# Splitting each weight once and keeping the split copy in DRAM scratch

## The chip, the cores and the metric

The kernel runs on one core of a Trainium2 chip. The metric is device time in microseconds (us). Three executions of the kernel before took 1098.61, 1100.31 and 1105.79 us; the median is 1100.31 us.

## What is computed

One encoder layer over two groups of tokens, a prompt of 1024 and a sample of 512, with 1024 channels each. Cut to what matters:

```python
h = rmsnorm(x, norm_g)
z = h @ w_in                                   # 1024 -> 4096 channels
hy_in, hy_gate, att_qkv, att_gate = split(z)
x0, x1, vv = split(short_conv(hy_in))
y_hy  = x0 * long_conv(x1 * vv, kfilt, hy_bias)            # FFT convolution
y_hy  = rmsnorm(y_hy, on_hy) * silu(hy_gate)
y_att = neighbourhood_attention(rmsnorm(q), rmsnorm(k), v, rpb)
y_att = rmsnorm(y_att, on_att) * silu(att_gate)
return x + concatenate([y_hy, y_att]) @ w_out
```

Both groups go through the same weights `w_in` and `w_out`, so every piece of a weight is used twice.

## The kernel before

TensorE multiplies in fp32r, a rounded float32. To keep float32 accuracy each operand is split into `hi` (the rounded value) and `lo` (what rounding left, rounded in turn), and each product is three matmuls: hi·hi, hi·lo, lo·hi. Weights arrive in pieces of [128, 1024] float32 (512 KB): 20 pieces of `w_ch` (channel-major projections, L392), 12 of `w_tk` (token-major ones, L405) and 8 of `w_out` (L1111). Each piece is split into two units, each a pair of tiles `whi`, `wlo` of [128, 512].

For each unit `issue_w` rounds half of the raw piece into `whi` (L365) and GpSimd subtracts `whi` from the raw half into `wlo` (L366). Rounding is done on ScalarE for the prompt (`self.w_round`), and on VectorE from the sample on. A pool has 2 raw buffers and 4 of `whi` and of `wlo`. `fetch_w` loads the raw piece behind the next one ahead of time. Since a piece is used once for the prompt and once for the sample, it is loaded and split twice: 80 loads, 160 roundings, 160 subtractions.

The work comes in five phases. `plan` fixes from the counts of steps how generators take turns, and with that the order of the weights: (1) filters' spectra beside q, k, v of the prompt; (2) hyena of the prompt; (3) attention of the prompt beside all projections and hyena of the sample; (4) output projections of the prompt and the first half of the sample's, beside the attention of the sample; (5) the second half of the sample's output. In the profile phase 3 takes about 535 to 885 us, phases 4 and 5 the time from there. In phase 4 `out_part` runs as `out0` and `out1` for the prompt and `out0` for the sample, four pieces of `w_out` each, and from `more_w` on the units come from two pools in turn. Within each phase a scheduler with a timing model of its own sets the order of instructions on each engine. Every DMA is issued by SyncE (SP) in that order and on one queue: an issue that waits holds up all behind it.

Other lines that come up: T and Ti are the bias tables of the attention, summed on GpSimd (L63) from `qkr`, which is loaded from `in_rpb`; `hThi_s`, `hTlo_s` are the sample's operands, loaded at the start of phase 3; L79 is a multiplication by a scalar on VectorE.

Of the kernel before, what the change touches and what calls it, by code (L numbers as in the profile page):

```python
# [49 lines left out]
class Kernel:  # L50
# [6 lines left out]
    # ---------------------------------------------------------------- helpers  # L57
# [28 lines left out]
    def psum(self, side, keep=0, **banks):  # L86
        """Share the banks of one side out anew, but for its first keep pools: tag -> number of banks."""
# [11 lines left out]
    # ------------------------------------------------------------------ setup  # L99
    def setup(self):  # L100
# [6 lines left out]
        self.w_pos, self.w_raw, self.w_ready, self.w_bufs = 0, [], [], 4  # L107
        self.dr = ctx.enter_context(self.pool("dr", space=bass.MemoryType.DRAM))
# [19 lines left out]
        # DRAM scratch  # L128
# [57 lines left out]
    def stack(self, out, src):  # L186
        """The halves of the partitions of src, split: hi in their own place and lo on the other half."""
        for d in range(2):
            r, o = slice(d * 64, d * 64 + 64), slice(64 - d * 64, 128 - d * 64)
            self.nc.scalar.copy(out=out[d][r], in_=src[r])  # L190
            self.sub(out[d][o], src[r], f32(out[d][r]))

    def w3_load(self, pool):
        """The last weights of the filters: per half of the partitions hi on both halves, and lo in its place."""
# [8 lines left out]
    def rsqrt(self, pool, ss, n, scale, name):  # L203
        """(ss * scale + eps) ** -0.5 for a [P, n] tile."""
# [13 lines left out]
    # ------------------------------------------------------------ input norm  # L218
    def x_norm(self, G, xp, ahead):
        """The rows of x, scaled by their rms."""  # L220
# [18 lines left out]
    def x_turn(self, G, hps):  # L239
        """Channel-major copies of the normed x, split into hi and lo."""  # L240
# [12 lines left out]
    def x_pre(self, G, pool):  # L253
        """Channel-major copies of the normed x, split into hi and lo, to scratch."""
# [39 lines left out]
    # --------------------------------------------------------------- weights  # L294
    def steps(self, what):
        """The pieces of the weights that each step of a generator takes."""
# [19 lines left out]
    def merge(ns, spans):  # L316
        """The order in which generators of ns[i] steps take turns, each spread evenly over its span."""
# [3 lines left out]
    def plan(self, phases):  # L321
        """phases: lists of (names of chained generators, span, priority).  Sets the order of the weights."""
# [9 lines left out]
    def weave(self, *gens):  # L332
        """Trace the generators of the next phase in turns."""
# [10 lines left out]
    def fetch_w(self):  # L344
        """Load the next [P, 1024] piece."""
        if self.w_pos < len(self.w_seq):
# [3 lines left out]
            raw = pool.tile([P, 1024], F32, name="wraw", bufs=2)  # L350
            self.dma(raw, self.io[key[0]][key[1:]])
            self.w_raw.append((key, raw, pool))

    def issue_w(self):
        """Split the next piece into two units of (hi, lo) [P, 512]; the piece behind it is on its way."""
        nc = self.nc
        if not self.w_raw:
            self.fetch_w()
        key, raw, pool = self.w_raw.pop(0)
        self.fetch_w()  # L360
        for u in range(2):
            hi = pool.tile([P, 512], F32R, name="whi", bufs=4)
            lo = pool.tile([P, 512], F32R, name="wlo", bufs=4)
            r = raw[:, u * 512:(u + 1) * 512]
            next(self.w_round)(out=hi, in_=r)  # L365
            nc.gpsimd.tensor_tensor(out=lo, in0=r, in1=f32(hi), op=ALU.subtract)  # L366
            self.w_ready.append((key, hi, lo))

    def take_w(self, key):
        """The next unit of piece key; pieces behind it are fetched as far as there is room."""  # L370
# [8 lines left out]
    def proj_ch(self, G, *gis):  # L379
        """128 output channels of each granule of gis, channel-major: per granule a list of psum [P, 512].  # L380
        The granules take turns in each segment of tokens."""
# [13 lines left out]
    def proj_tok(self, gi, hi, lo, nt):  # L395
        """256 output columns, token-major, for nt (<=8) token tiles.  Returns list of psum [P, 4, 256]."""
# [1005 lines left out]
```

## Time and profile before

| | |
|---|---|
| runs | 1098.61, 1100.31, 1105.79 us, median 1100.31 us |
| profiled execution, first to last instruction | 1101.3 us (the only time recorded for it) |
| PE busy | 1030.7 us, 94% |
| DVE, ACT, POOL busy | 824.4, 561.1, 539.9 us |
| moved by DMA | 154.87 MB, mean 141 GB/s |
| mean granted TensorE clock | 0.987 |

PE is TensorE, DVE VectorE, ACT ScalarE, POOL GpSimd, SPq the queue of SyncE. PE is busy nearly throughout, so what a change to the other engines is worth is found in the gaps of PE: what each gap waits for, and how the granted clock moves around it.

### The profile page before, as it was taken

What the parts mean: (1) busy time and instruction counts of PE and PEld (TensorE: products, weight loads), DVE (VectorE), ACT (ScalarE), POOL (GpSimd) and SP (SyncE); (2) the same over time, 40 slices, a digit from 0 to 9 for tenths busy, and PEclk for the clock granted to TensorE, in tenths of its full rate; (3) what the DMA queues carried; (4) which work ended last, traced back from release to release, by engine and by line L of the source; (5) the groups of instructions that cost most, each with busy time, mean ns of one, the idle gap of its engine ahead of it and who ended that gap; (6) DMA issues with size and microseconds to landing.
All of it is one profiled execution on the core that took longest, in us unless ns stands there. A gap on an engine that the chain in (4) does not pass through costs nothing. (4 is left out here: it accounts for less than half of the span.)

```text
span 1101.3 us, 18549 instructions
## 1 busy us (share of the span) xinstructions
PE 1030.7 (94%) x6492; PEld 895.6 (81%) x6492; DVE 824.4 (75%) x2098; ACT 561.1 (51%) x1223; POOL 539.9 (49%) x480
## 2 busy tenths in 40 slices
PE   3999898998999999999898999999999999899998
PEld 2888887987888878787786887888777798798898
DVE  5988679456148597868768898999886868966874
ACT  6644616444534343443425577667567764564530
POOL 2133636325245474545445645455455564766452
PEclk9999999899999999999999899999999999999999
DMA  9134461645612121122375244445544376966522
GB/s 343 34 122 144 143 207 61 219 150 164 224 39 74 46 79 54 50 72 77 118 227 173 78 129 146 120 141 182 140 129 138 114 243 190 321 203 205 164 76 89
DMA packets 110780, 154.87 MB, mean 141 GB/s; under 512 B 7793, under 2 KB 80315, under 8 KB 109919
## 3 DMA queue, kind: packets, MB, share of 16 engines
q1 hardware_dynamic: 110687, 153.69, 44.3%
q8 instruction: 51, 0.84, 0.3%
q14 instruction: 42, 0.34, 0.1%
HBM read 110.35 MB, written 43.32 MB: 140 GB/s over the span
## 5 line engine op out<-in xcount | busy, mean ns | idle before, releaser
L366 POOL TENSOR_TENSOR wlo<-wraw,whi 128x512 fp32r<-128x512 f32 x160 | 231.5, 1451 | 308.4 <-ACT whi L365 180.7
L392 PE MATMUL bank<-hThi_p,whi 128*128 128x512 f32 x320 | 125.2, 391 | 2.0 <-DVE cx L75 2.0
L392 PE MATMUL bank<-hTlo_p,whi 128*128 128x512 f32 x320 | 125.5, 392 | 0.0
L392 PE MATMUL bank<-hThi_p,wlo 128*128 128x512 f32 x320 | 125.4, 392 | 0.0
L405 PE MATMUL bank<-whi,hThi_p 128*128 128x256 f32 x384 | 110.4, 290 | 2.5 <-ACT qsq L849 2.0
L1111 PE MATMUL bank<-whi,hi 128*128 128x256 f32 x384 | 111.0, 291 | 0.8 <-ACT hi L1090 0.5
L405 PE MATMUL bank<-wlo,hThi_p 128*128 128x256 f32 x384 | 110.8, 291 | 0.0
L1111 PE MATMUL bank<-wlo,hi 128*128 128x256 f32 x384 | 110.0, 288 | 0.0
L1111 PE MATMUL bank<-whi,lo 128*128 128x256 f32 x384 | 109.5, 289 | 0.3 <-POOL lo L63 0.3
L405 PE MATMUL bank<-whi,hTlo_p 128*128 128x256 f32 x384 | 108.1, 289 | 0.0
L450 POOL TENSOR_TENSOR Z<-zc,Z 128x256 fp32r<-128x256 f32 x80 | 69.5, 878 | 49.2 <-ACT Z L449 36.2
L1002 ACT ACTIVATE s_sb<-s_sb,mx 128x360 f32<-128x360 f32 (+1 forms) x96 | 60.4, 629 | 63.6 <-DVE mx L998 63.0
L405 PEld LDWEIGHTS bank<-whi,hThi_p 128*128 128x128 f32 x384 | 74.2, 194 | 4.9 <-ACT qsq L849 2.4
L1111 PEld LDWEIGHTS bank<-whi,hi 128*128 128x128 f32 x384 | 73.4, 191 | 4.1 <-issue 2.1
L405 PEld LDWEIGHTS bank<-wlo,hThi_p 128*128 128x128 f32 x384 | 74.5, 194 | 1.6 <-issue 0.7
L1111 PEld LDWEIGHTS bank<-wlo,hi 128*128 128x128 f32 x384 | 73.6, 192 | 1.6 <-issue 1.6
L1111 PEld LDWEIGHTS bank<-whi,lo 128*128 128x128 f32 x384 | 73.1, 192 | 1.7 <-issue 1.1
L405 PEld LDWEIGHTS bank<-whi,hTlo_p 128*128 128x128 f32 x384 | 73.3, 194 | 1.2 <-issue 0.7
L392 PEld LDWEIGHTS bank<-hThi_p,whi 128*128 128x128 f32 x320 | 60.3, 188 | 14.0 <-DVE cx L75 2.4
L392 PEld LDWEIGHTS bank<-hTlo_p,whi 128*128 128x128 f32 x320 | 60.4, 189 | 11.3
L392 PEld LDWEIGHTS bank<-hThi_p,wlo 128*128 128x128 f32 x320 | 60.3, 188 | 11.3
L392 PE MATMUL bank<-hThi_s,whi 128*128 128x512 f32 x160 | 64.6, 407 | 4.4 <-DVE cvv L75 2.3
(292 smaller groups left out, 3108.4 us busy)
## 6 DMA issues: line engine op xcount, KB each, us to landing
wraw<-in_w_ch_dram SPq DMA_DIRECT2D x40, 512.0 KB
wraw<-in_w_tk_dram SPq DMA_DIRECT2D x24, 512.0 KB
wraw<-in_w_out_dram SPq DMA_DIRECT2D x16, 512.0 KB
V<-v_p SPq DMA_DIRECT2D x32, 240.0 KB
v_p<-vg SPq DMA_DIRECT2D x32, 160.0 KB
K_p<-Kw SPq DMA_DIRECT2D x4, 1088.0 KB
x<-in_x_prompt_dram SPq DMA_DIRECT2D x8, 512.0 KB
dec<-in_dec_p_dram SPq DMA_DIRECT2D x16, 256.0 KB
```

The lines of the kernel that those rows point to most:

```text
L366: nc.gpsimd.tensor_tensor(out=lo, in0=r, in1=f32(hi), op=ALU.subtract)
L392: nc.tensor.matmul(ps, lhsT=w, rhs=h[s][:, k], start=(k == 0 and i == 0), stop=(k == KC - 1 and i == 2))
L405: nc.tensor.matmul(pss[t // 2][:, t % 2, :], lhsT=h[t // 4][:, k, t % 4 * P:(t % 4 + 1) * P], rhs=w, start=(k == 0 and i == 0 and t % 2 == ...
L450: nc.gpsimd.tensor_tensor(out=Z[:, 1, 0:2, :], in0=z, in1=f32(Z[:, 0, 0:2, :]), op=ALU.subtract)
L1002: nc.scalar.activation(out=s_sb[:, :n], in_=s_sb[:, :n], func=AF.Exp, bias=mx, scale=-1.0, accum_out=l)
L1111: nc.tensor.matmul(ps[:, j, :], lhsT=h[:, tok], rhs=w, start=(k == 0 and i == 0 and j == 0), stop=(k == 3 and i == 2 and j == 1))
```

## The change

At the first use of a piece each unit is split as before, now into the two halves of one tile `wsp` [128, 2, 512], and that tile is also written to a DRAM tile `ws_...` of 512 KB, if the piece comes again. At the second use no raw piece is loaded: each unit is loaded ready from its DRAM tile, into buffers of tag `wsp` or, every third, `wraw`. So a pool holds 4 units at first use and 6 at second use; `w_bufs`, which limits how far `take_w` runs ahead, goes from 4 to 6 with phase 3 and from 8 to 10 in phase 4. In numbers: 80 subtractions on GpSimd and 80 roundings (78 on VectorE, 2 on ScalarE) go; 40 loads of 512 KB become 80 loads of 512 KB; 80 stores of 512 KB are added, 64 of them before phase 3 and 16 from its end on.

```diff
     def fetch_w(self):
...
-            raw = pool.tile([P, 1024], F32, name="wraw", bufs=2)
-            self.dma(raw, self.io[key[0]][key[1:]])
+            raw = None
+            if key not in self.w_split:
+                raw = pool.tile([P, 1024], F32, name="wraw", bufs=2)
+                self.dma(raw, self.io[key[0]][key[1:]])
             self.w_raw.append((key, raw, pool))
 
     def issue_w(self):
...
         key, raw, pool = self.w_raw.pop(0)
+        kept = self.w_split.get(key)
+        if kept is None:
+            kept = self.w_split[key] = [self.dr.tile([P, 2, 512], F32, name="_".join(["ws", *map(str, key), str(u)])) for u in range(2)]
         self.fetch_w()
         for u in range(2):
-            hi = pool.tile([P, 512], F32R, name="whi", bufs=4)
-            lo = pool.tile([P, 512], F32R, name="wlo", bufs=4)
-            r = raw[:, u * 512:(u + 1) * 512]
-            next(self.w_round)(out=hi, in_=r)
-            nc.gpsimd.tensor_tensor(out=lo, in0=r, in1=f32(hi), op=ALU.subtract)
-            self.w_ready.append((key, hi, lo))
+            if raw is None:
+
+                tag = next(self.w_tags.setdefault(id(pool), itertools.cycle(["wsp", "wsp", "wraw"])))
+                t = pool.tile([P, 2, 512], F32R, name=tag, bufs=2 if tag == "wraw" else 4)
+                self.dma(f32(t), kept[u])
+            else:
+                t = pool.tile([P, 2, 512], F32R, name="wsp", bufs=4)
+                r = raw[:, u * 512:(u + 1) * 512]
+                next(self.w_round)(out=t[:, 0], in_=r)
+                self.nc.gpsimd.tensor_tensor(out=t[:, 1], in0=r, in1=f32(t[:, 0]), op=ALU.subtract)
+                if key in self.w_seq[self.w_pos:]:
+                    self.dma(kept[u], f32(t))
+            self.w_ready.append((key, t[:, 0], t[:, 1]))
...
         self.w_round = itertools.repeat(self.nc.vector.tensor_copy)
+        self.w_bufs = 6
...
-            self.w_pools, self.w_bufs = itertools.cycle((wp, self.wp)), 8
+            self.w_pools, self.w_bufs = itertools.cycle((wp, self.wp)), 10
```

The other lines of the diff only drop comments. The scheduler makes a new order of it. Three places in it matter below. The first is on GpSimd near the start of phase 3, where the first bias tables are summed; before:

```order
L63 TENSOR_TENSOR cx_6422<-cx_6422,cvv 128x512
L366 TENSOR_TENSOR wlo<-wraw,whi 128x512 x3
L63 TENSOR_TENSOR T_6350<-cmask,qkr 128x480
L63 TENSOR_TENSOR T_6353<-cmask,qkr 128x480
L63 TENSOR_TENSOR Ti_6352<-T_6350,rmask 128x480
L63 TENSOR_TENSOR Ti_6355<-T_6353,rmask 128x480
L366 TENSOR_TENSOR wlo<-wraw,whi 128x512
L470 TENSOR_TENSOR Z<-zc,Z 128x256
```

There a weight's subtraction stands behind four sums of the tables. The same place after:

```order
L63 TENSOR_TENSOR cx_6478<-cx_6478,cvv 128x512
L63 TENSOR_TENSOR T_6406<-cmask,qkr 128x480
L63 TENSOR_TENSOR T_6409<-cmask,qkr 128x480
L483 TENSOR_TENSOR Z<-zc,Z 128x256
L463 TENSOR_TENSOR Z<-zc,Z 128x256
L63 TENSOR_TENSOR Ti_6408<-T_6406,rmask 128x480
```

The tables remain, and no work on weights stands behind them. The second place is the queue of SP at the change from phase 2 to 3, up to the first loads of the sample's operands (`Kc` are spectra of filters, `ga_p` gates that are stored); before:

```order
L60 DMA wraw<-in_w_tk_dram 128x1024
L60 DMA Kc<-K_p_93 128x256
L60 DMA wraw<-in_w_tk_dram 128x1024
L60 DMA Kc<-K_p_93 128x256 x4
L60 DMA hThi_s<-hT_76 128x1024
L60 DMA ga_p_89<-vg 128x1024
L60 DMA hTlo_s<-hT_77 128x1024
```

Two raw pieces stand well ahead of the sample's operands. The same place after:

```order
L60 DMA wsp<-ws_w_ch_0_3311 128x1024
L60 DMA wsp<-ws_w_ch_1_3312 128x1024
L60 DMA Kc<-K_p_93 128x256 x3
L60 DMA wsp<-ws_w_tk_0_1_190 128x1024
L60 DMA Kc<-K_p_93 128x256
L60 DMA wsp<-ws_w_tk_1_0_240 128x1024
L60 DMA hThi_s<-hT_76 128x1024
L60 DMA ga_p_89<-vg 128x1024
L60 DMA hTlo_s<-hT_77 128x1024
```

Four loads of units, each into a buffer that TensorE must have left, are now mixed into the last loads ahead of them. The third place is the queue of SP in phase 4 around the loads of the sample's rows (`acc`) and of the prompt's partial sums (`oy`); before:

```order
L60 DMA wraw<-in_w_out_dram 128x1024 x2
L60 DMA ox<-in_x_prompt_dram 128x2x256
L60 DMA V<-v_s_122 120x3x128
L60 DMA qkr<-in_rpb_dram 128x1x488
L60 DMA ox<-in_x_prompt_dram 128x2x256
L60 DMA lo_12507<-A_s_105 128x512
L60 DMA acc<-in_x_sample_dram 128x4x256 x4
```

After, at the same loads:

```order
L60 DMA ws_w_out_0_0_10839<-wsp 128x1024
L60 DMA sum<-oo 128x2x256
L60 DMA acc<-in_x_sample_dram 128x4x256 x3
L60 DMA qkr<-k_s_120 128x4x128
L60 DMA acc<-in_x_sample_dram 128x4x256
L60 DMA ws_w_out_0_1_10840<-wsp 128x1024
L60 DMA wraw<-in_w_out_dram 128x1024
L60 DMA oy<-sum 128x2x256
L60 DMA ox<-in_x_prompt_dram 128x2x256
L60 DMA wsp<-ws_w_out_0_0_10378 128x1024
L60 DMA wsp<-ws_w_out_0_1_10379 128x1024
```

Stores of units, each behind its own subtraction, now stand among the loads, and units of the second use are fetched there too.

## Rows read from the trace of the kernel before

**Rows 1.** The page, part 1: busy us, share of the span, instructions.

```profile
PE 1030.7 (94%) x6492; PEld 895.6 (81%) x6492; DVE 824.4 (75%) x2098; ACT 561.1 (51%) x1223; POOL 539.9 (49%) x480
```

**Rows 2.** Windows by stage: length, busy PE, PEld, DVE, ACT, POOL; clock, DMA share, GB/s.

```profile
0.00:535.00 535.00, 493.74 (x2970) 430.02 (x2971) 370.51 (x963) 246.88 (x550) 235.36 (x206) 0.99 0.36 119
535.00:885.00 350.00, 333.44 (x1989) 277.98 (x1988) 299.28 (x759) 217.28 (x452) 183.31 (x164) 0.98 0.49 147
885.00:1101.30 216.30, 203.53 (x1536) 187.55 (x1534) 154.64 (x378) 96.90 (x222) 121.20 (x112) 0.99 0.60 184
```

**Rows 3.** Lines L365 and L366: durations in ns, min/median/max, first and last start.

```profile
L365 DVE CAST whi<-wraw x94: 398/422/1560, 536.9 to 1074.3; 128x512 fp32r<-128x512 f32 x94
...
L366 POOL TENSOR_TENSOR wlo<-wraw,whi x160: 1261/1296/5379, 10.9 to 1075.8; 128x512 fp32r<-128x512 f32 x160
```

**Rows 4.** Windows of line L365 alone: length, busy DVE, busy ACT; clock, DMA share, GB/s.

```profile
535.00:885.00 350.00, 39.88 (x66) 0.00 (x0) 0.98 0.49 147
885.00:1101.30 216.30, 14.71 (x28) 0.00 (x0) 0.99 0.60 184
```

**Rows 5.** Waits of PE, 535 to 885 us: us in total, times, longest.

```profile
PE bank L405 <- POOL wlo L366: 3.9, 2, 2.8
PE bank L392 <- DVE cvv L75: 2.3, 1, 2.3
PE bank L392 <- DMA hThi_s<-hT: 2.1, 1, 2.1
...
PE bank L405 <- DVE whi L365: 0.3, 1, 0.3
...
PE bank L405 <- ACT vg L849: 0.2, 1, 0.2
```

**Rows 6.** Waits of PE from 885 us on: first and last row.

```profile
PE bank L763 <- DVE s L63: 1.7, 1, 1.7
...
PE bank L945 <- DMA qkr<-q_s: 0.2, 1, 0.2
```

**Rows 7.** Timeline of POOL near 600 us: start, us, instruction, idle before and what ended it.

```profile
601.23 2.37 POOL L63 TENSOR_TENSOR T<-cmask,qkr 128x480 f32<-128x480 f32 x2 [5.37 <-DMA qkr<-in_rpb_dram]
...
605.45 1.26 POOL L366 TENSOR_TENSOR wlo<-wraw,whi 128x512 fp32r<-128x512 f32 x1
```

**Rows 8.** Windows of 5 us there, columns as in Rows 2.

```profile
600.00:605.00 5.00, 3.11 (x18) 2.04 (x16) 1.84 (x5) 1.40 (x4) 3.77 (x4) 1.00 0.19 67
605.00:610.00 5.00, 3.23 (x15) 3.23 (x16) 2.56 (x3) 0.42 (x1) 4.38 (x5) 0.51 0.47 149
610.00:615.00 5.00, 5.00 (x29) 4.28 (x29) 4.41 (x18) 4.10 (x10) 1.05 (x2) 0.81 0.01 2
```

**Rows 9.** Timeline of 930 to 942 us: one form of L79 twice, and a subtraction.

```profile
930.87 0.41 DVE L79 TENSOR_SCALAR s_sb<-s_sb,rl 128x360 f32<-128x360 f32 x1
...
940.32 1.28 POOL L366 TENSOR_TENSOR wlo<-wraw,whi 128x512 fp32r<-128x512 f32 x1 [0.37 <-DVE rl L1004]
940.35 1.46 DVE L79 TENSOR_SCALAR s_sb<-s_sb,rl 128x360 f32<-128x360 f32 x1
```

**Rows 10.** Waits of SP's queue over the span, the longest in total.

```profile
SPq L60 <- POOL wlo L366: 275.3, 59, 22.3
```

**Rows 11.** DMA issues, the first group: times, KB each.

```profile
wraw<-in_w_ch_dram SPq DMA_DIRECT2D x40, 512.0 KB
```

**Rows 12.** Window at the start of phase 3, columns as in Rows 2.

```profile
545.00:560.00 15.00, 12.28 (x61) 10.67 (x61) 5.73 (x23) 2.70 (x8) 2.71 (x3) 0.77 0.91 332
```

**Rows 13.** Window of line L365 in phase 4, columns as in Rows 4.

```profile
930.00:970.00 40.00, 4.35 (x8) 0.00 (x0) 0.97 1.03 314
```

**Rows 14.** Chain that ended last, same stretch: start, us, what.

```profile
938.91 7.46 DMA ox<-in_x_prompt_dram
...
946.39 10.84 DMA acc<-in_x_sample_dram
...
957.29 7.31 DMA wraw<-in_w_out_dram
```

More of the change, by code (lines that the diff above doesn't have):

```diff
@@ L107, in setup @@
         self.w_pos, self.w_raw, self.w_ready, self.w_bufs = 0, [], [], 4
+        self.w_split, self.w_tags = {}, {}
         self.dr = ctx.enter_context(self.pool("dr", space=bass.MemoryType.DRAM))
@@ L349, in fetch_w @@
             pool = next(self.w_pools)
-            raw = pool.tile([P, 1024], F32, name="wraw", bufs=2)
-            self.dma(raw, self.io[key[0]][key[1:]])
+            raw = None
+            if key not in self.w_split:
+                raw = pool.tile([P, 1024], F32, name="wraw", bufs=2)
+                self.dma(raw, self.io[key[0]][key[1:]])
             self.w_raw.append((key, raw, pool))
     def issue_w(self):
-        nc = self.nc
         if not self.w_raw:
```

## Prediction, made before the run

> **What bounds the kernel now.** I read the page first, then windows by phase, then what PE waits for in each, then the places of the largest waits. PE is busy 94% of the span, DVE 75%, POOL 49% [rows 1]. PE's matmuls all stay, so only PE's gaps can be won, and the slow clock behind some of them. By phase [rows 2] PE is idle 41 us of 535 before phase 3, 16.6 of 350 in phase 3, 12.8 of 216 after it. All second uses of weights but one piece are split from 535 us on [rows 3, 4], so gains lie in these last two stretches. DVE is nearly as full as PE in phase 3: 299 of 350 us [rows 2]. The page's shares hide that: a wait of PE there is mostly a wait for something DVE or POOL was late with.
>
> PE's waits in phase 3 [rows 5] fall into three sorts. Split weights: 3.9 us for `wlo` (two waits, the longest 2.8 us) and 0.3 for `whi`. Loads of the sample's operands: 2.1 and 0.7 us (that second row, of `hTlo_s`, stands among those left out). Everything else from DVE, ACT and POOL: ten rows, from 2.3 us for `cvv` down to 0.2, together 9.4 us. From 885 us on the waits are small [rows 6]: 13 rows, of which DVE's six sum to 4.8 us and those on ACT and POOL to 1.7.
>
> **The change part by part.** I sum against the profiled execution, 1101.3 us; the median of the runs is 1.0 us less, which I subtract at the end.
>
> *The waits for split weights.* The largest is a matter of order. Near 600 us POOL stood 5.37 us for a table's operand, then worked through four sums of tables, and only then came to a `wlo` that PE needed, at 605.45 us [rows 7]. PE was idle 1.9 us before and 1.8 us after 605 us. Right after that the granted clock was 0.51 for 5 us and 0.81 for 5 more [rows 8]: part of the time at the lower of its two levels, 1.2 instead of 2.4 GHz. That cost 0.49 x 5 + 0.19 x 5 = 3.4 us beside the wait. In the new order no subtraction stands behind the tables there, and the second uses have none at all. All 4.2 us of these waits and the 3.4 us of clock go: -7.6 us. At the other end PE only meets the next late thing (DVE stood for the same tables): -2.
>
> *DVE and POOL unloaded in phase 3.* 62 of the 66 roundings go: 62/66 x 39.88 us = 37.5 us of DVE [rows 4], and as many subtractions of 1.3 us [rows 3] = 80 us of POOL. DVE gains more than the roundings: one form of L79 took 0.41 us at 930.87 and 1.46 us at 940.35, where it began 0.03 us behind a subtraction on POOL and ended just after it [rows 9]; the rounding itself has a median of 422 ns and a longest of 1560 [rows 3]. The Trainium skill, page "SBUF — State Buffer", section "Who interferes with whom", says that DVE and GpSimd share a pair of ports under an exclusive lock, and that the later of the two blocks for the whole instruction; the trace agrees (1.46 us beside 0.41). Between nothing and 1.1 us freed for each of 62 subtractions, I take half, 34 us. Then DVE is busy about 299 - 37 - 34 = 228 of 350 us. How much of the 9.4 us of waits that saves lies between 0 and 9.4: much of it is latency (a maximum, an exponential, a convolution behind the matmul that feeds it), not queueing. I take half: -4.7 us.
>
> *The same after 885 us.* Only 16 of 28 roundings are second uses: 16/28 x 14.71 = 8.4 us of DVE [rows 4] in a stretch where DVE is busy 155 of 216 us. Of the 4.8 us of waits on DVE I take a fifth, -1.0; bounds 0 and -6.5 (all on DVE, ACT and POOL).
>
> *Stores before phase 3.* 64 stores of 0.52 MB are 33.6 MB in 535 us, whose DMA share was 0.36 at 119 GB/s [rows 2]; by that ratio it becomes about 0.55. Each store waits on SP for its subtraction, and behind it on that queue stand loads of spectra, decays and raw weights. But SP already waits for the same subtractions, 275 us in 59 waits [rows 10], since a raw load needs the buffer that a subtraction empties; the store waits at the same point. A `wsp` buffer comes free only when its store has read it, some us after the subtraction, while PE keeps it longer than that. I take +1 (0 to +5).
>
> *The change from phase 2 to 3.* Here the second use costs something new. Raw pieces could lie ready in buffers of their own; ready units must go into buffers that PE has left. So the last loads of units stand directly ahead of the sample's operands on SP, the last two just before and after the last `Kc` load, and PE has nothing else to do there: it waited 2.1 and 0.7 us for these operands [rows 5], and between 545 and 560 us the DMA engines were 0.91 busy at 332 GB/s with PE's clock at 0.77 [rows 12]. Two units are 1.05 MB, at 332 GB/s 3.2 us later for the first operand; four units would be 6.3. I take +3.3 (0 to +6.3).
>
> *Loads in phase 3.* 31 pieces cost 1.05 MB instead of the 512 KB of a raw load [rows 11]: 16 MB more in 350 us, 147 to 194 GB/s, share 0.49 to 0.65 [rows 2]. A unit has up to four others ready ahead of it, over 15 us of PE work at 350 us for 32 pieces. I take +1 (0 to +5).
>
> *Loads and stores in phase 4.* From 930 to 970 us DMA is saturated: share 1.03 at 314 GB/s, and 8 units are split just there [rows 13]. They are first uses of the second half of `w_out`, so 8 stores of 0.52 MB join: 4.2 MB, 13.4 us at 314 GB/s; four loads of second uses, 0.52 MB larger each, would make that 6.3 MB and 20 us. The chain runs through DMA there: 7.5 us to an `ox`, 10.8 to `acc`, 7.3 to a raw weight [rows 14]. Yet PE has attention to do meanwhile and loses only 12.8 us after 885 us in all [rows 2]. Bounds 0 and +20; since PE's waits for DMA in that stretch are at most a few tenths each [rows 6], I stay near the low end: +3.
>
> Sum: -7.6 - 4.7 - 1.0 + 1 + 3.3 + 1 + 3 = -5.0, so 1096.3 for the span and **1095 us** for the median.
>
> **The rivals.** *B: the relief is whole.* Waits in phase 3 are mostly queueing on DVE and POOL, prolonged by the subtractions that hold up DVE. Then all 9.4 and 6.5 us go with the 7.6, DMA costs no more than the 1 us for stores, and the time is 1101.3 - 23.5 + 1 - 1.0 = 1078. The 86% of DVE in phase 3 and L79's two durations speak for it; against it, that half of the waits are on steps with latency of their own. The page on SBUF, by its lock, would side with B.
>
> *C: nothing comes of it.* PE meets the next late engine where `wlo` was late, DVE's free time falls into gaps that PE doesn't see, and DMA takes the rest: 1097 to 1103, centre 1100. For it: PE is already busy 333 of 350 us [rows 2].
>
> *D: DMA bounds phase 4, slower than before.* The place is the queue of SP around `acc` and `oy`, which now stand behind stores. The price is up to 20 us; it decides once the lag of the DMA engines exceeds what loads have in hand. The raw weight of 957 us had nothing in hand: the chain passes through its landing [rows 14]. With the other terms as above: 1095 - 3 + 20 = 1112; with half the lag, 1102. For it: the share of 1.03 [rows 13]. Against: less is moved before and after, and weights are fetched deeper. That the change doesn't do what it says is excluded: 80 subtractions and 78 of DVE's roundings are gone from the order.
>
> **How the numbers follow.** The forecast, 1088 to 1100, has 0.42; B (below 1088) 0.23; C (1097 to 1103 without the gains) 0.19; D (above 1103) 0.16. A measurement of this kernel can tell about 1%, 11 us, from no change: faster means below 1089.3, slower above 1111.3. Faster: B and the edge of the forecast, 0.33. Slower: the larger part of D, 0.10. Same: 0.57. For 8 in 10 I leave out the ends of B and D: 1079 to 1110.
>
> **What would show each step.** In the profile after: no wait of PE on a subtraction in phase 3 and a clock of 1.00 where the first tables are summed (else the first term is wrong); waits on DVE in phase 3 of some 5 us in total, with DVE near 230 of 350 us; a wait of some 5 to 6 us for `hThi_s` at the start of phase 3; phases 1 and 2 as long as before within 2 us; a DMA share of 1 from about 930 to 985 us, with waits of PE for DMA of no more than 3 us more. The forecast fails if PE waits long for a `wsp` load in phase 3 (its prefetch too shallow behind a blocked SP), or if the new order of the scheduler makes a gap that none of these rows shows.

## Result, and the profile after

The changed kernel takes 1112.7 us (median of 4 runs, 1109.5 to 1114.3) where the kernel before takes 1099.5; the ratio is 1.011, 95% interval 1.008 to 1.015. It is slower by about 1%; forecast were 1095 us and a range up to 1110. The profiled execution has a span of 1111.5 us against 1101.3.

The page, part 1, answers to [rows 1]. DVE is 57 us shorter and POOL 115 us, so the splits are gone. PE's work has not changed and its share falls.

```profile
PE 1033.8 (93%) x6492; PEld 902.2 (81%) x6492; DVE 767.1 (69%) x2020; ACT 560.4 (50%) x1219; POOL 424.5 (38%) x400
```

Windows by stage answer to [rows 2] (columns: length; busy PE, PEld, DVE, ACT, POOL; granted clock, DMA share, GB/s), and those of the rounding's line alone, now L376, to [rows 4].

```profile
0.00:535.00 535.00, 484.36 (x2912) 420.86 (x2912) 366.03 (x944) 242.09 (x537) 223.75 (x199) 0.99 0.52 181
535.00:885.00 350.00, 337.36 (x2031) 283.42 (x2032) 256.81 (x717) 216.94 (x460) 100.03 (x107) 0.98 0.64 197
885.00:1111.50 226.50, 212.08 (x1552) 197.90 (x1550) 144.24 (x362) 101.42 (x223) 100.75 (x95) 0.95 0.72 230
```

```profile
535.00:885.00 350.00, 1.25 (x3) 0.00 (x0) 0.98 0.64 197
```

PE lost 9.4 us of work before 535 us, where DMA is far from full (0.52). Which waits are they? All waits of PE from 500 to 570 us (us in total, times, longest):

```profile
PE bank L474 <- ACT Z L482: 5.7, 1, 5.7
PE bank L405 <- DVE cx L75: 5.4, 1, 5.4
PE bank L405 <- DMA hThi_s<-hT: 4.6, 1, 4.6
PE bank L475 <- POOL Z L483: 1.6, 1, 1.6
PE bank L405 <- DMA hTlo_s<-hT: 1.1, 1, 1.1
```

None is for a split or a load of a unit. Three of the five, 12.6 us before rounding, lie at the end of phase 2; before the change the waits at the same places are 0.5 us for `Z` and 2.0 for `cx`. PE's timeline there (start, length, instruction, idle before and what ended it) shows that it runs out of projections on `hThi_p`, does a few small transforms of the last long convolution as DVE, ACT and POOL deliver them, and stands:

```profile
522.64 0.39 PE L405 MATMUL bank<-hThi_p,wsp 128*128 128x512 f32 x1
528.70 0.58 PE L474 MATMUL bank<-Z,fc 128*128 128x256 f32 x1 [5.67 <-ACT Z L482]
...
531.27 0.58 PE L475 MATMUL bank<-Z,fc 128*128 128x256 f32 x1 [1.59 <-POOL Z L483]
...
539.13 0.80 PE L405 MATMUL bank<-hThi_p,wsp 128*128 128x512 f32 x1 [5.36 <-DVE cx L75]
```

The window around it, first after, then before, shows which engine is full while PE stands: DVE is busy 19 of 20 us. The granted clock of the stretch is 0.67: from the first gap on, part of it ran at the lower of the two levels.

```profile
520.00:540.00 20.00, 7.38 (x28) 5.70 (x27) 19.05 (x50) 8.21 (x18) 8.77 (x7) 0.67 0.09 34
```

```profile
520.00:540.00 20.00, 17.99 (x99) 15.35 (x99) 14.90 (x39) 9.62 (x24) 11.54 (x14) 1.00 0.14 46
```

In the order of instructions, 107 projection matmuls of the prompt stood on PE behind the transposes that begin the last convolution (`cx`) before the change; now 62 do. The rest has been issued earlier, and the convolution begins 13 us later: its transposes start at 506 us before and at 519 now. Of these matmuls, 59 stood ahead of the wait for `cx` before, and 14 do now; the other 48 stand behind it in both and cover nothing of it.

From here on I cut the span at two instructions instead of at fixed times. One is the first matmul on the sample's operands (`hThi_s`); "first" is how late it is against before (547.3 us). In the kernel before the other is the last matmul on them, from which on 1570 of PE's 6492 matmuls are left. In another order that last matmul stands elsewhere (1533 left in the changed kernel), so I cut every kernel where 1570 are left. "Phase 3" is the time between the two cuts (332.4 us before), "rest" the time from the second to the end of the span (221.6). They are starts in the profiled executions. As matmuls differ in size, phase 3 and rest are good to some 1.5 us where PE's order is not that of before, in e6 and e7 to 2.5; ratios are of the timed runs.

| kernel | ratio to before | first | phase 3 | rest |
|---|---|---|---|---|
| after | 1.011 (1.008 to 1.015) | +18.5 | 315.7 | 230.0 |
| e1 one tile | 1.026 (1.023 to 1.028) | +10.3 | 346.4 | 223.7 |
| e2 stores only | 1.040 (1.037 to 1.044) | +16.6 | 345.5 | 236.3 |
| e3 loads only | 0.999 (0.997 to 1.001) | +13.0 | 314.6 | 223.8 |
| e4 stores on GpSimd's queue | 1.020 (1.017 to 1.024) | +25.0 | 315.6 | 230.2 |
| e5 one tile, old depths | 1.023 (1.020 to 1.027) | +6.0 | 335.0 | 234.9 |
| e6 two tiles | 1.018 (1.014 to 1.023) | +14.5 | 324.2 | 238.5 |
| e7 another plan | 1.019 (1.016 to 1.023) | +23.0 | 318.8 | 231.0 |
| e8 only w_tk | 1.002 (0.9995 to 1.004) | +4.4 | 325.6 | 223.8 |
| e9 change, old order | 0.999 (0.997 to 1.0015) | +4.7 | 320.0 | 223.1 |
| e10 before, new order | 1.015 (1.011 to 1.019) | +14.0 | 332.9 | 220.1 |
| e11 two tiles, old order | 1.011 (1.007 to 1.014) | +11.7 | 331.8 | 231.8 |
| e12 e11 without w_out | 1.003 (1.001 to 1.005) | +3.5 | 328.1 | 220.4 |
| e13 loads only, old order | 0.993 (0.991 to 0.995) | +2.9 | 322.5 | 223.1 |
| e14 old order to phase 2 | 0.997 (0.995 to 0.999) | +8.4 | 317.7 | 223.1 |
| e15 only w_ch, old order | 0.997 (0.995 to 0.999) | -5.7 | 328.0 | 224.6 |
| e16 no w_out, old order | 1.001 (0.999 to 1.004) | +11.9 | 322.0 | 224.8 |
| e17 e15, bound to phase 2 | 1.003 (1.001 to 1.005) | -3.3 | 332.3 | 224.0 |

So the changed kernel is 18.5 us late when phase 3 begins, wins 16.7 us in it, and loses 8.4 behind it.

### The profile page after: what moved, and what is told of

Its sections match the earlier page's. It is cut to its first block, busy times and chain, and to the rows that moved or that the text cites. A ratio compares the mean times of both kernels' runs of the same rounds, so it can differ in the third digit from the quotient of the medians.

```text
span 1111.5 us, 18535 instructions
## 1 busy us (share of the span) xinstructions
PE 1033.8 (93%) x6492; PEld 902.2 (81%) x6492; DVE 767.1 (69%) x2020; ACT 560.4 (50%) x1219; POOL 424.5 (38%) x400
## 4 chain that ended last, share of the span: by engine, by line
PE 61%; DVE 18%; DMA 9%; ACT 5%; issue 3%; POOL 3%; SPq 1%; POOLq 0%; DVEq 0%; ACTq 0%
PE bank L405 20%; PE bank L418 11%; PE bank L1124 11%; PE bank L1042 3%; PE bank L1033 3%; DMA qkr<-in_rpb_dram 2%; DMA v_p<-vg 2%; PE bank L1008 2%; DVE zc L63 2%; PE bank L474 2%; PE bank L475 2%; PE bank L476 2%; PE bank L1007 1%; DVE oO L75 1%; DVE s L63 1%
## 5 line engine op out<-in xcount | busy, mean ns | idle before, releaser
L405 PE MATMUL bank<-hThi_p,wsp 128*128 128x512 f32 x640 | 205.0, 395 | 11.3 <-DVE cx L75 5.8
L377 POOL TENSOR_TENSOR wsp<-wraw,wsp 128x512 fp32r<-128x512 f32 x80 | 117.4, 1472 | 227.2 <-ACT wsp L376 151.3
L418 PE MATMUL bank<-wsp,hThi_p 128*128 128x256 f32 x768 | 149.6, 288 | 2.9 <-ACT qsq L862 2.5
L405 PEld LDWEIGHTS bank<-hThi_p,wsp 128*128 128x128 f32 x640 | 120.2, 190 | 36.2 <-DVE cx L75 6.5
L1124 PE MATMUL bank<-wsp,hi 128*128 128x256 f32 x688 | 139.8, 299 | 3.9 <-ACT hi L1103 2.1
L418 PEld LDWEIGHTS bank<-wsp,hThi_p 128*128 128x128 f32 x768 | 121.8, 193 | 6.2 <-ACT qsq L862 2.9
L405 PE MATMUL bank<-hTlo_p,wsp 128*128 128x512 f32 x320 | 126.1, 394 | 0.0
L1124 PEld LDWEIGHTS bank<-wsp,hi 128*128 128x128 f32 x688 | 113.7, 202 | 6.9 <-issue 2.3
L418 PE MATMUL bank<-wsp,hTlo_p 128*128 128x256 f32 x384 | 108.6, 290 | 0.0
L1124 PE MATMUL bank<-wsp,lo 128*128 128x256 f32 x344 | 100.0, 296 | 0.4 <-POOL lo L63 0.4
L376 ACT CAST wsp<-wraw 128x512 fp32r<-128x512 f32 x64 | 39.2, 617 | 56.3 <-PE bank L418 38.2
```

Source lines behind the costliest of these rows:

```text
L376: next(self.w_round)(out=t[:, 0], in_=r)
L377: self.nc.gpsimd.tensor_tensor(out=t[:, 1], in0=r, in1=f32(t[:, 0]), op=ALU.subtract)
L405: nc.tensor.matmul(ps, lhsT=w, rhs=h[s][:, k], start=(k == 0 and i == 0), stop=(k == KC - 1 and i == 2))
L418: nc.tensor.matmul(pss[t // 2][:, t % 2, :], lhsT=h[t // 4][:, k, t % 4 * P:(t % 4 + 1) * P], rhs=w, start=(k == 0 and i == 0 and t % 2 == ...
L1124: nc.tensor.matmul(ps[:, j, :], lhsT=h[:, tok], rhs=w, start=(k == 0 and i == 0 and j == 0), stop=(k == 3 and i == 2 and j == 1))
```

## The experiments

**One tile, stores, loads, another queue.** The first four take the change apart. In e1 and e2 the pieces are loaded raw at both uses (`if True:`); e1 leaves the stores out, e2 makes each once; e3 stores one unit alone; e4 moves the stores. (What the expectations of e1 and e2 call the last sums are the transposes of `cx`.)

```diff
 # e1, e2
-            if key not in self.w_split:
+            if True:
 # e1
-                if key in self.w_seq[self.w_pos:]:
-                    self.dma(kept[u], f32(t))
 # e3
-                self.dma(f32(t), kept[u])
+                self.dma(f32(t), self.w_one[0])
 # e4
-                    self.dma(kept[u], f32(t))
+                    self.nc.gpsimd.dma_start(out=kept[u], in_=f32(t))
```

> Weights are split at both uses as before, nothing is stored or loaded; of the change only the common tile of hi and lo (wsp) and the depths 6 and 10 are kept. In the order this leaves 79 matmuls of the prompt's projections on TensorE behind the last sums of phase 2 (cx), against 107 before and 62 in the changed kernel. Theory O (the order starves TensorE at the end of phase 2): a part of the gap near 525 to 540 us is there, about 28/45 of it, 5 to 8 us, so 1104 to 1108. Theory S (the stores themselves delay loads on SP and the release of buffers): phases 1 and 2 as before, 1097 to 1102. Theory P (the loss is made in phase 4 by transfers): 1097 to 1102 too.

> The 80 stores are made, but the second uses are split anew from the raw weights; nothing of the scratch is read. No relief in phase 3 and no change at the handover. Order as in the changed kernel: 62 matmuls behind the last cx. S: phases 1 and 2 lose the 13 us that they lose in the changed kernel by 500 us, 1110 to 1118 at the end. O: the gap at the end of phase 2 as in the changed kernel, but before 500 us nothing that the order does not explain: 1106 to 1114. Theory H (the loss is at the handover, where ready units are loaded in front of the sample's operands): 1098 to 1103, and the first matmul on the sample's operands at most 6 us later than before. P: phase 4 loses only what 8 stores cost, 1100 to 1104.

> Two stores alone are made (one unit at the start), and every second use reads that one unit, so the second uses compute with wrong weights: the relief and the loads of the second uses without the stores. Order: 79 matmuls behind the last cx. S: phases 1 and 2 as before, the relief of 8 us in phase 3 stays, and only the handover's 5 us is lost: 1092 to 1098. O: the gap at the end of phase 2 costs 5 to 8 us, 1098 to 1104. H: the wait for hThi_s of 4 us or more and the 5 us behind it are unchanged; 1100 or more. P (loads in phase 4): phase 4 loses its 10 us as in the changed kernel, 1100 to 1105.

> As the changed kernel, but the stores are issued from GpSimd's queue, right behind the subtraction that they wait for, and no longer stand on SP. The same bytes are moved. Order: 85 matmuls behind the last cx. S, by SP's queue: the first matmul on the sample's operands is 5 to 8 us late instead of 18, and the time 1098 to 1103. S, by bytes and held buffers: as the changed kernel, 1108 to 1114. O: about half of the gap is left, 1103 to 1108.

Measured: 1128.9, 1146.0, 1100.4 and 1122.2 us. Only e3 lies within a range given for it (those of O, H and P hold it); e1, e2 and e4 are slower than any of theirs. All four begin phase 3 late, e1 too, which moves not one byte more than before: 10.3 us. That speaks for O and against S and H as the main cause. But e1 lost far more than O gave it: its phase 3 is 14 us longer than before's. With the splits of the second uses taken out of it (e3 against e1) phase 3 is 32 us shorter. So a common tile, depths 6 and 10 and the scheduler's new order make a kernel that is much worse than the one before, and the loads repair most of that. The 79 stores of e3 to after cost 12 us, partly in a worse order (79 to 62 matmuls left). e4's hope fell: with the stores on GpSimd's queue the kernel is slower than with them on SP's and 25 us late at phase 3; by 138 us, in the stretch of the filters' spectra, PE has issued 774 matmuls, against 787 in the changed kernel and 825 before. Its order is another too, so this isn't the queue's price alone.

**Tile or depth; two tiles; another plan; w_tk alone.** e5 is e1 with the depths of before. e6 and e8 give hi and lo tiles of their own. e7 changes one number of the plan.

```diff
 # e5, e6, e8
-        self.w_bufs = 6
...
-            self.w_pools, self.w_bufs = itertools.cycle((wp, self.wp)), 10
+            self.w_pools, self.w_bufs = itertools.cycle((wp, self.wp)), 8
 # e6, e8
+            hi = pool.tile([P, 512], F32R, name="whi", bufs=4)
+            lo = pool.tile([P, 512], F32R, name="wlo", bufs=4)
...
+                self.dma(f32(hi), kept[u][:, 0])
+                self.dma(f32(lo), kept[u][:, 1])
 # e7
-            [(["hyena_p"], every, 0), (["ga_c"], (0.8, 1.0), 0)],
+            [(["hyena_p"], every, 0), (["ga_c"], (0.92, 1.0), 0)],
```

> As e1 (one common tile for hi and lo, split at both uses, no stores, no loads), but with the depths of before: up to 4 and 8 units ready instead of 6 and 10. Order at the end of phase 2 as in e1. Theory M (the common tile costs: a matmul that reads hi waits for the subtraction too, and a buffer of hi is held until lo has been read): as e1, 1125 to 1131. Theory D (the depth of 6 costs: six units are split ahead into four buffers, so a rounding waits for TensorE at the head of DVE's queue): the 20 us that e1 lost in phase 3 are gone, 1104 to 1110. In both the first matmul on the sample's operands stays 8 to 12 us late.

> As the changed kernel, but hi and lo have tiles of their own (4 buffers each), each stored and loaded by a transfer of its own of half the size, and the depths are those of before, 4 and 8. 71 matmuls of the prompt's projections are left behind the transposes that begin the last convolution of phase 2 (107 before, 62 in the changed kernel). M: the first matmul on the sample's operands comes 10 us earlier than in the changed kernel, 1098 to 1104. O (the order at the end of phase 2 alone makes that loss): 71 is as poor as 62, so 15 us or more late there, 1108 to 1114. S (stores): 12 us over the same without stores, 1105 to 1112.

> As the changed kernel, but one number of the plan is changed: the gates at the end of phase 2 take their turns in the last 8 per cent of the phase instead of the last 20, which leaves 96 matmuls of the prompt's projections for the last convolution instead of 62 to 89. All stores and loads are as in the changed kernel. O: the gap of 12 us from 525 to 540 us goes down to 3 or less, 1101 to 1106. M and S: the gap stays by 8 us or more or appears elsewhere before the first matmul on the sample's operands, 1109 to 1115.

> Only the pieces of w_tk are kept (24 pieces of 2 units at most, stored in phase 1, loaded in phase 3); w_ch and w_out are split twice as before; two tiles and the depths of before. The order at the end of phase 2 is that of before, 107 matmuls left. O and P: no loss in phases 2 and 4, 2 to 5 us at the handover, and of the relief in phase 3 the larger part, 6 to 10 us: 1092 to 1098. S: the stores of phase 1 still cost 3 to 5 us by 250 us and the handover 5: 1098 to 1105.

Measured: 1126.2, 1122.0, 1122.7 and 1103.2 us. The total of e5 lies in M's range. Its phase 3 takes 335.0 us instead of e1's 346.4, which D would explain by the depth of 6 with only four buffers to split into; the order of phase 3 changed with the depth, so this isn't shown. The total hardly moved, because the rest became 11 us longer; why, no run here settles. e6 speaks against M: with two tiles phase 3 still begins 14.5 us late; its total is above every range. e7, above every range as well, seems to refute O: 96 matmuls left, and still 23 us late. But PE's timeline shows where these 96 stand. Between the transposes and the wait for `Z` PE has no projection at all, and up to `cx` only small transforms:

```profile
515.70 0.85 PE L776 MATMUL bank<-ident,xu 128*128 128x128 f32 x3
525.84 0.58 PE L474 MATMUL bank<-Z,fc 128*128 128x256 f32 x1 [9.29 <-ACT Z L482]
```

All 96 stand behind the wait for `cx`. So the count to take is that of the projections ahead of that wait. Counted so, every run falls into line (PE's waits for `Z` and `cx` behind the last transposes, summed):

| kernels | projections ahead of the wait for `cx` | waits, us |
|---|---|---|
| before, e8, e9, e11 to e17 | 59 | 2.5 |
| e4 | 37 | 7.6 |
| e1, e3, e5 | 31 | 9.0 |
| e6 | 23 | 10.7 |
| after, e2, e10 | 14 | 12.6 |
| e7 | 0 | 16.2 |

That is 0.23 us of waiting for each projection that is missing, whatever else the kernel loads or stores. e8, whose order there is that of before, begins only 4.4 us late and wins some 5 to 7 us in phase 3, but its total is level with before, in S's range and above that of O and P. (Of w_tk there are 12 pieces and 24 units, not 24 pieces as its expectation says.)

**The order alone.** These runs hold the work fixed and exchange the order. The other version is traced first; then every engine is bound to issue its instructions in that version's order, except the steps of splitting.

```diff
+        by = {tags[i.name]: i for i in traced if i.name in tags}
+        for eng in ENGINES:
+            last = None
+            for tg in like[eng]:
+                i = by.get(tg)
...
+                if last is not None:
+                    tc.add_manual_dep(i, last.name, mybir.DependencyInfo(
+                        mybir.DependencyClass.NoSync, mybir.DependencyReason.DATA), reason="order")
+                last = i
```

> All work of the changed kernel (common tile, depths 6 and 10, 80 stores, all loads of units), but TensorE (up to about 20 us into phase 4), VectorE, ScalarE and GpSimd are bound to issue everything that is not a step of splitting in the order of the kernel before; only the splits, the stores and loads, SP's queue and the end of TensorE's order are the scheduler's. So 107 matmuls are left for the last convolution of phase 2. Theory O (the loss is the order's): no gap at 525 to 540 us, the first matmul on the sample's operands 3 to 8 us later than before instead of 18, the relief of 8 to 11 us in phase 3 as in the changed kernel: 1090 to 1100. Theory S (stores delay what stands behind them): that first matmul is 10 us late or more, 1102 to 1110. Theory M (the common tile): the same lateness, 8 to 10 us before the end of phase 2, but without stores to blame: 1103 to 1110.

> All work of the kernel before (two tiles, split at both uses, no stores, no loads of units), but in phases 1 and 2 the four engines are bound to the order of the changed kernel; from phase 3 on the scheduler decides. O: the gap at the end of phase 2 (waits for the transposes' operand Z and for cx, 12 us) is there although nothing is stored or loaded, and the first matmul on the sample's operands comes 8 to 15 us later than before. S and M: it comes within 3 us of before, since what they blame is not in this kernel. The total is that plus what the scheduler makes of phases 3 and 4, 1100 to 1120.

> As e9, but with tiles of their own for hi and lo, each stored and loaded by its own transfer, the depths of before, and the whole of TensorE's order bound to that of before. O: as e9 or better by up to 5 us, 1086 to 1098. M: better than e9 by 5 to 10 us. S: 1100 to 1110. Theory P (the loads and stores of phase 4 delay it): 885 us to the end takes 5 to 10 us longer than before, so 1096 to 1104.

> As e11, but w_out is not kept and is split at both of its uses as before; so phase 4 does what it did before, in the order of before. P: 5 to 10 us shorter than e11. O, where phase 4 lost by its order only: within 3 us of e11. In both theories O and P this is the fastest of all, 1086 to 1096, if the handover costs no more than 5 us; by S 1098 to 1105.

Measured: 1099.9, 1115.5, 1113.5 and 1104.5 us. e9 and e10 came out as O expected and decide it. With all its work but the order of before, the change is level with before (by the ratio -0.9 us, interval -3.4 to +1.7). With the work of before but the new order in phases 1 and 2, the kernel before is 1.5% slower, some 14 to 16 us; from phase 3 on its order came out as before's, and phase 3 and rest take as long as there. The two differences from before, -0.9 us for the work and about +14 for the order, add up to about the changed kernel's +13 (1112.7 against 1099.5). Waits of PE in e10 from 500 to 570 us, and the window:

```profile
PE bank L504 <- ACT Z L512: 5.7, 1, 5.7
PE bank L435 <- DVE cx L77: 5.4, 1, 5.4
PE bank L505 <- POOL Z L513: 1.6, 1, 1.6
PE bank L435 <- DMA hThi_s<-hT: 1.3, 1, 1.3
PE bank L435 <- DMA hTlo_s<-hT: 0.2, 1, 0.2
```

```profile
520.00:540.00 20.00, 7.38 (x27) 5.64 (x26) 19.07 (x50) 8.20 (x18) 8.78 (x7) 0.63 0.09 33
```

The same three waits to a tenth of a us, PE busy the same 7.38 us, without a store or a load of a unit. In e9 they are down to the 2.5 us of before, and the wait for the sample's operands is the longest that is left:

```profile
PE bank L435 <- DMA hThi_s<-hT: 5.0, 1, 5.0
PE bank L435 <- DVE cx L77: 2.0, 1, 2.0
PE bank L505 <- POOL Z L513: 0.5, 1, 0.5
PE bank L806 <- DVE xu L65: 0.3, 1, 0.3
```

```profile
520.00:540.00 20.00, 17.49 (x94) 14.63 (x93) 14.31 (x42) 10.38 (x25) 9.77 (x11) 1.00 0.39 120
```

M as the cause of the gap is refuted by this pair: e10 has tiles of their own for `hi` and `lo` and has the gap, e9 has the common tile and does not. e11 and e12 speak against M too: two tiles with the depths of before are worse than e9, and e11 is slower than every range given for it, e12 in S's. At the start of phase 3 PE then waits for units, which no wait of e9 shows (e11, 545 to 890 us):

```profile
PE bank L443 <- DMA whi<-ws_w_tk: 6.6, 3, 2.9
PE bank L430 <- DMA hThi_s<-hT: 4.8, 1, 4.8
PE bank L430 <- DMA whi<-ws_w_ch: 2.9, 1, 2.9
```

This points to the depth of 6, with room for two more units in the raw buffers, as the better one for loads; as e11 differs from e9 also in its tiles and in twice as many transfers of half the size, it isn't shown by itself. e11 to e12 also shows 9 us for w_out, but e16 shows no such gain at depth 6.

**Where the old order wins nothing, and what beats both.**

```diff
 # e13, on e9: as e3
 # e14, e17: bound only as far as phase 2
-CUT = {"EngineType.PE": 5400}
+CUT = {"EngineType.PE": 3020, "EngineType.DVE": 960, "EngineType.Activation": 484, "EngineType.Pool": 130}
 # e15, e17, on e9
-        if kept is None:
+        if kept is None and self.keep and key[0] == "w_ch":
...
-                if self.keep and key in self.w_seq[self.w_pos:]:
+                if self.keep and key[0] == "w_ch" and key in self.w_seq[self.w_pos:]:
 # e16: the same with key[0] != "w_out"
```

> As e9 (the change in the order of before), but one unit alone is stored and every second use loads that one, so that second uses compute with wrong weights. It differs from e9 by 79 stores. If the stores are what e9 still loses (3 to 5 us by 300 us, and up to 2 in phase 4): 1093 to 1097, and at 300 us within 1 us of before. Rival: e9's lateness in phases 1 and 2 is not made by the stores; then as e9, 1098 to 1102.

> The changed kernel, bound to the order of before in phases 1 and 2 alone; phases 3 and 4 are ordered by the scheduler. Theory O1 (all that the new order costs is at the end of phase 2): within 3 us of e9, 1097 to 1103. Theory O2 (the scheduler's order of phases 3 and 4 costs too, as the 15 us suggest that the changed kernel loses between 855 us and the end): 1104 to 1112, with phase 4 the longer by it.

> As e9, but only w_ch is kept: 40 stores, nearly all in phase 2, where the DMA engines' share was 0.26, and 38 of the 62 units that phase 3 split anew are loaded; w_tk and w_out are split twice. If the stores of phase 1 and the loads of w_tk at the handover are what e9 loses: at 300 us within 1 us of before, the first matmul on the sample's operands at most 2 us late, and 38/62 of the 12.4 us that e9 won in phase 3, 7.6 us: 1092 to 1097, faster than e9 and before. Rival: what e9 wins in phase 3 hangs on w_tk's units, split in the stretch where GpSimd sums tables: then 1098 to 1102.

> As e9 (common tile, depths 6 and 10), but w_out is split at both uses: 64 stores, none in phase 4. P: the 1.5 us that e9 loses after 885 us come back, 1096 to 1100. If depth alone was why e12 (the same with two tiles and depth 4) fell back by 7 us at the start of phase 3, its first 50 us of phase 3 are as in e9, within 2 us.

> The two that were faster than before, put together: only w_ch is kept, with 40 stores (as e15), and the order of before is bound in phases 1 and 2 alone, phases 3 and 4 are the scheduler's (as e14). If both gains are independent (e14 was 2.5 us below e9, e15 3.7): 1092 to 1096. If the scheduler's order of phase 3 is good only with all units loaded, since 24 units of w_tk are split again in it, with up to six ahead in four buffers as in e1: 1097 to 1110.

Measured: 1091.8, 1097.4, 1096.2, 1101.5 and 1102.9 us. Without stores the change in the old order is 0.7% faster than before; e9 is 0.1% faster. So the stores take 0.6%, about 6.5 us, of a gain of some 7.4 (e13 also reads one and the same 512 KB at every second use, which this difference includes). S was right that stores cost something, and wrong that they make the gap. e14 shows O1: binding phases 1 and 2 alone is enough, the scheduler's own order of phases 3 and 4 costs nothing there. It changes the changed kernel by one thing, the order of its first half, and makes it 15 us faster (1112.7 to 1097.4). In the profiled executions 10.1 us of that lie before phase 3. Another 6.9 lie in the rest, where both issue the same matmuls in the same order; first after, then e14:

```profile
881.50:1111.50 230.00, 215.58 (x1571) 200.46 (x1569) 146.02 (x368) 102.54 (x225) 100.75 (x95) 0.95 0.72 230
```

```profile
873.40:1096.50 223.10, 209.25 (x1571) 193.63 (x1569) 144.42 (x368) 102.05 (x225) 101.76 (x95) 0.98 0.74 237
```

PE is idle for 14 us in either; what differs is the granted clock, 0.95 against 0.98. Why it does is open.

e15 beats both kernels too, by 0.3% over before. Its phase 3 of 328.0 us is 4.4 us shorter than before, less than the 7.6 expected, and begins 5.7 us earlier; both figures are shifted by a wait of 4.5 us for `hTlo_s`, which stands right behind its first matmul on the sample's operands, while e9 waits 5.0 us right ahead of it. P fell with e16: no gain without w_out. The first 250 matmuls of e16's phase 3 take 49.6 us, e9's 49.0 and e12's 53.5, so e12's loss there goes with its depth or its two tiles. e17 shows that e14's and e15's gains do not add up: in the scheduler's order w_tk's splits make PE wait for `wsp` 4.3 us in phase 3, against 1.9 in e15.

## Why the prediction was wrong

Its own steps, against the changed kernel and against e9, which has the order that the prediction reckoned with:

| step | forecast | after | e9 |
|---|---|---|---|
| lateness at the first sample matmul (stores +1, change of phase +3.3) | +4.3 | +18.5 | +4.7 |
| phase 3 (waits for splits -7.6, unloading -4.7, loads +1) | -11.3 | -16.7 | -12.4 |
| after it (-1.0 and +3) | +2.0 | +8.4 | +1.5 |
| span | -5.0 | +10.2 | -6.1 |

The agreement of e9's span with the forecast is luck. A timed execution is 1.7 to 2.0 us longer than its span in every run, so the profiled execution of before would have been timed at about 1103 us, above its medians of 1099.5 to 1101.7, and e9's, at 1096.9, is 3.0 below its own. By the ratio of the timed runs e9 wins 0.9 us, not 6.1.

**The step that failed** is the one that allowed only the stores to act before phase 3 (bounds 0 to +5) and so expected phases 1 and 2 "as long as before within 2 us". The price of the new order there was left out: 14.0 us in e10, the whole sign of the result. The prediction ended on "the new order of the scheduler makes a gap that none of these rows shows", but gave that no term, no chance and no rival. It could have been seen before the run: PE fills the wait for the last convolution with projections, and the new order left 14 of them ahead of `cx` instead of 59. In the trace of before a projection starts every 0.23 us there (506.54, then 506.77), so 45 fewer are 10 us of cover less; measured are 10.1 us more of waiting (12.6 against 2.5).

**The split weights' waits** went as forecast. No wait for a split stands in phase 3 of the changed kernel, and the clock is 1.00 from 600 to 640 us, where its first tables are summed (from 614 us) and [rows 8] had 0.51:

```profile
600.00:640.00 40.00, 40.00 (x240) 33.08 (x238) 30.33 (x73) 26.69 (x56) 15.75 (x17) 1.00 0.65 210
```

The forecast counted some of the clock's price twice: PE was busy for only 3.23 of the 5 us at 0.51, so it is 0.49 x 3.23 + 0.19 x 5 = 2.5 us beside the wait, not 3.4. All waits of PE from 565 to 885 us beside those for the sample's operands are:

```profile
PE bank L1042 <- ACT pt L1035: 1.1, 1, 1.1
PE bank L405 <- ACT vg L899: 0.5, 1, 0.5
PE bank L418 <- DVE vg L63: 0.4, 1, 0.4
PE bank L475 <- POOL Y L679: 0.3, 1, 0.3
PE bank L418 <- ACT vg L862: 0.3, 1, 0.3
```

They sum to 2.6 us, where [rows 5] have 9.4 without the splits. So 6.8 of the 9.4 went: between the half that was taken and the whole of rival B.

**The unloading of DVE** was mis-sized, without harm to the sum. e9 can be laid beside before row by row, since between the same two matmuls it issues the same 1893 on TensorE (columns as in the windows above; before from 547.3 us, then e9 from 552 us):

```profile
547.30:879.70 332.40, 318.27 (x1893) 265.32 (x1894) 283.90 (x718) 207.16 (x431) 174.49 (x155) 0.98 0.49 145
```

```profile
552.00:872.00 320.00, 314.12 (x1893) 263.96 (x1894) 234.57 (x649) 206.70 (x431) 92.13 (x95) 0.99 0.64 199
```

DVE falls by 49.3 us, and its roundings there by 36.8 (38.1 to 1.3). That leaves 12.5. As roundings partly overlap other records of DVE, the busy time of all its other instructions falls by more, 19 us (252.8 to 233.5). Some 3 us of either are nine instructions fewer in the stretch. So some 9 to 16 us, not 34, are what VectorE gains with 60 subtractions fewer beside it, about 0.2 us for each. Instructions of one form show it: of the L79 of [rows 9] in this stretch of before, six of the eight that overlapped a subtraction took 1.1 to 1.4 us, and the five beside no work of GpSimd 0.39 to 0.41. The rule of the Trainium skill, page "SBUF — State Buffer", section "Who interferes with whom", that the later of the two engines blocks for the whole instruction, agrees with these durations in kind. Half of 1.1 us for every subtraction was too much, though; and in e9 four of the eight L79 of this form that overlapped work of GpSimd still took 1.1 to 1.4 us.

**The change of phase** came as forecast: waits of 4.6 and 1.1 us for the operands, 5.7 together against 2.8 before, and in e9 5.0.

**The stores** are the second step that failed, a term too small: before phase 3 they were put at +1 with +5 as the bound, and behind it they are part of the +3. Runs e9 and e13 give 6.5 us for 79 of them over the whole kernel. So even in the order of before the change won 0.9 us (-1.7 to 3.4) instead of the forecast 5. The profiled executions can't divide the 6.5 us among the phases, for the reason in the last section.

**Rival D**, at 1112, named the right time by luck. DMA is saturated as forecast:

```profile
930.00:970.00 40.00, 36.34 (x257) 32.60 (x256) 30.61 (x69) 22.41 (x50) 27.39 (x25) 0.96 1.02 346
```

Still no wait of PE for a DMA is in the rows after 885 us. The rest of the kernel is 8.4 us longer, not 20, with a granted clock of 0.95 against 0.99 before; e14, with the same loads and stores there and a DMA share of 0.74 against 0.72, is 1.5 us longer.

Open are four things: why e5's rest is 11 us longer than e1's, why the clock of the changed kernel's rest is lower than e14's, why the scheduler's order of phases 3 and 4 serves e14 and not e17, and what in the scheduler's reckoning makes it issue the projections of phase 2 early; that it does so with the common tile alone (79) is shown, not why.

## What to carry to other kernels

Where a scheduler sets the order, a change has two effects: its own, and that of the order that comes out. Price them apart: before the run by comparing the order at the places where filler covers a latency (count the filler ahead of the wait, not all that is left), and on the chip by binding the new work to the old order and the old work to the new one. Ten of the seventeen variants here were slower than the kernel before by more than their intervals; a single slow variant therefore says little about an idea. Here the idea is worth 0.3% in a good order (e14, e15; intervals 0.1 to 0.5%), and would be worth 0.7% if its stores were free.

## What the runs showed of the hardware

In some executions TensorE's clock fell without any idle time in the rows before it. Windows of 5 us in e16, where PE is busy for 5.00 us in every window from 45 to 95 us:

```profile
75.00:80.00 5.00, 5.00 (x31) 3.82 (x29) 3.47 (x9) 1.47 (x4) 4.10 (x5) 1.00 0.82 256
80.00:85.00 5.00, 5.00 (x20) 4.16 (x19) 1.73 (x4) 0.21 (x1) 0.00 (x0) 0.52 1.02 348
85.00:90.00 5.00, 5.00 (x16) 3.66 (x16) 0.69 (x1) 0.41 (x1) 1.27 (x1) 0.50 1.05 374
```

The lower of the two levels, 1.2 GHz, is held in both windows, and PE issues 36 matmuls in them instead of before's 69. The profiled executions of e11, e13, e14 and e16 have it (0.50 to 0.52 from 80 to 90 us). Eight others have 1.00 there, and before too; the other six have 0.66 to 0.73 in the first of the two windows and 0.92 to 1.00 in the second. e13 has it without the stores and with DMA at 0.85 and then 0.33, so a full DMA does not make it; e9, with the same order and the stores, has 1.00 and DMA at 1.06. What makes it is open. How much later it makes "first" no row shows by itself; the profiled executions of these four took 0.8 (e14) to 10.9 us (e11) more than their medians, e16's 1107.8 us against 1101.5, e13's 1097.5 against 1091.8. A difference of that size between single profiles proves nothing; the ratios do.
